# Forming the low halves of the first 80 expert-weight tiles with an accumulating DMA in place of a VectorE subtraction

## The chip, the cores and the metric

The kernel runs on one core of one Trainium2 chip. The metric is the device time of one execution in microseconds (us); lower is better. The engines are TensorE (PE; its weight loads PEld), VectorE (DVE), ScalarE (ACT), GpSimd (POOL) and SyncE (SP), with 16 DMA engines beside them. ACT, POOL and SP also issue DMAs, each on a queue of its own.

## The reference, cut to what matters

The whole program is one block with an SSM branch, an attention branch and a PEER layer, followed by two further blocks, on 512 tokens of width 1024. The change lies in the PEER layer: every token picks 128 of 16384 experts, and each expert is a row of `u_tab` and a row of `v_tab`.

```python
def one_block(args):
    h_blk, i_blk, g_blk = args
    u_sel = u_tab[i_blk]
    act = jax.nn.gelu(jnp.einsum('td,thkd->thk', h_blk, u_sel).astype(jnp.float32))
    w = (g_blk * act).astype(h.dtype)
    return jnp.einsum('thk,thkd->td', w, v_tab[i_blk])
```

## The kernel before, in words

Matrix products are done in fp32r, a rounded fp32, and made exact enough by splitting each operand into a high part (rounded) and a low part (what the rounding lost). `mm3` (L327 to L330) adds three products: high by high (L328), high by low and low by high (L329, L330).

All weights come through one `Stream`. `_load` (L64 to L68) has SP issue the load of a 128x1024 f32 tile `wraw` (512 KB). `_split` (L70 to L77) makes `whi` on ACT (L75, a copy that rounds) and `wlo` on DVE (L76, `wraw - whi`). The tags `wraw`, `whi` and `wlo` have three buffers each. `get` (L79) splits up to two tiles ahead of the one asked for and loads ahead of that. So the split of tile i+2 waits until PE has finished with tile i-1, and the load of tile i+3 waits until tile i is split.

The PEER layer (`peer`, from L915) treats 384 of the tokens densely: for each of 128 tiles of 128 experts it computes the products of all tokens with all rows of U, and weights them with a gate matrix that is zero where an expert was not picked. The other 128 tokens are treated by gathering their rows with indirect DMAs (`gathered`, L965 to L996, an indirect DMA on POOL at L975 and a dot product on DVE at L984).

- The U stage: after the 16 query tiles, `spill(e)` (L1131) runs for e = 0 to 71: one U tile, 24 matmuls (`u_pass`, L960), a Gelu on ACT (L1137) and, every fourth tile, a store of the results to memory (`at`, L1139). Behind each, `tick(0, ...)` (L1144) takes two steps of the gate work, and `tick(1, ...)` a quarter of a step of the gathered lane.
- The gate work: `prep(t)` (L1022) sorts and decodes the picks of 128 tokens, almost all of it on DVE. `build(t)` (L1091) then has 32 steps per block: two comparisons on DVE (L1099, L1100, tiles `o1` and `o2`), a product on POOL (L1101, `og`), eight matmul instructions (L1104) and a copy on ACT (L1105); every eight steps a 2 MB store goes out (L1107, `gt`). The lane does prep(0), prep(1), then build(1) beside prep(2), build(2) beside prep(3), and build(3): 96 build steps in all, and what is left over after e = 71 is drained (L1145).
- Eight late U tiles (L1173, e = 72 to 79) follow, and then the V stage: 128 tiles of V and the 48 remaining tiles of U.

Instructions are placed on each engine's queue in the order of a scheduler's estimate when the program is built, and each engine then works its queue in order. `self.last` (L76) keeps the last low-part subtraction: `tick` ties the DVE instructions of the gathered lane behind it (L1126).

Of the kernel before, what the change touches and what calls it, by code (L numbers as in the profile page):

```python
# [13 lines left out]
AF = mybir.ActivationFunctionType  # L14
ALU = mybir.AluOpType
# [15 lines left out]
N_SPILL = 80  # L31
# [23 lines left out]
class Stream:  # L55
# [14 lines left out]
    def _split(self, i):  # L70
        r = self.raw.pop(i)
        hi = self.pool.tile([P, 1024], F32R, tag="whi", bufs=3, name=f"whi{i}")
        lo = self.pool.tile([P, 1024], F32R, tag="wlo", bufs=3, name=f"wlo{i}")
        w = self.specs[i][3] if len(self.specs[i]) > 3 else 1024
        self.nc.scalar.copy(hi[:, :w], r[:, :w])  # L75
        self.last = self.nc.vector.tensor_sub(lo[:, :w], r[:, :w], hi[:, :w])  # L76
        self.parts[i] = (hi, lo)  # L77

    def get(self, key, ahead=None):  # L79
# [1934 lines left out]
```

## Time and profile before

| | |
|---|---|
| median of 3 runs | 3367.07 us (3360.56 to 3369.22) |
| the profiled execution | 3364.15 us |
| its span, first to last instruction | 3362.4 us |
| granted TensorE clock, mean over the span | 0.977 |
| first U matmul | 584.2 us |
| first and last gate matmul | 730.0 and 1029.0 us |
| first V matmul | 1061.2 us |

Times inside the profile count from the first instruction. The views group instructions by line, engine and shape, with the busy time, the mean of one, and the idle time before it together with what ended it; or they give the busy time of each engine in a stretch. A granted clock of 1.00 is 2.4 GHz, of 0.5 is 1.2 GHz.

### The profile page before, as it was taken

How to read it: one execution, taken by the hardware profiler on the slowest of the kernel's cores; microseconds unless marked ns; L12 is line 12 of the kernel's file. 1: busy time of each engine (PE TensorE's matmuls, PEld its weight loads, DVE VectorE, ACT ScalarE, POOL GpSimd, SP SyncE). 2: the span in 40 equal slices, each digit the busy share in tenths (PEclk: the TensorE clock that was granted, in tenths of full speed). 3: DMA queues.
4: the chain of work that ended last, by engine and by line, in shares of the span. 5: the costliest groups of instructions: out<-in, count | busy, mean ns of one | idle time of the engine just before them, and what ended most of it. 6: DMA issues, size and time to landing. Idle time of an engine off the chain costs nothing.

```text
span 3362.4 us, 46297 instructions
## 1 busy us (share of the span) xinstructions
PE 3174.1 (94%) x17267; PEld 2756.3 (82%) x17267; DVE 2277.1 (68%) x4416; ACT 1344.6 (40%) x2494; POOL 833.3 (25%) x911
## 2 busy tenths in 40 slices
PE   7989999988988999999999996999999999999999
PEld 6988878988987777799998985878888986778887
DVE  6886359999995777788888688743324387753322
ACT  4445233433433333333334454632222377742222
POOL 1451000024554655566664110000000110000000
PEclk9999999999999999999999997999999998999999
DMA  4223332455657999999998221022223210122232
GB/s 139 78 77 112 100 114 85 154 189 200 236 216 277 344 324 332 327 338 335 340 335 295 81 73 42 31 85 97 95 94 130 78 51 1 57 63 95 99 94 82
DMA packets 226417, 529.25 MB, mean 157 GB/s; under 512 B 19080, under 2 KB 113160, under 8 KB 224272
## 3 DMA queue, kind: packets, MB, share of 16 engines
q1 hardware_dynamic: 186448, 376.32, 33.1%
q0 software_dynamic: 36864, 134.23, 11.0%
q10 hardware_dynamic: 2880, 15.73, 1.2%
q8 instruction: 136, 2.23, 0.3%
q14 instruction: 89, 0.73, 0.1%
HBM read 474.17 MB, written 51.40 MB: 156 GB/s over the span
## 4 chain that ended last, share of the span: by engine, by line
PE 56%; DVE 5%; DMA 3%; ACT 2%; issue 1%; POOL 1%; SPq 0%; ACTq 0%; DVEq 0%; POOLq 0%
PE mm L329 15%; PE mm L330 15%; PE mm L328 15%; PE ax L328 2%; PE ax L329 2%; PE ax L330 2%; DMA wraw<-in_peer_v_dram 2%; DVE wlo L76 1%; DMA rw<-in_peer_v_dram,idx 1%; PE tx L1279 1%; PE tx L1839 1%; ACT whi L75 1%; DVE tl L272 1%; PE sx L1819 0%; PE po L1849 0%
## 5 line engine op out<-in xcount | busy, mean ns | idle before, releaser
L76 DVE TENSOR_TENSOR wlo<-wraw,whi 128x1024 fp32r<-128x1024 f32 x525 | 682.6, 1300 | 557.4 <-ACT whi L75 550.7
L75 ACT CAST whi<-wraw 128x1024 fp32r<-128x1024 f32 x525 | 549.6, 1049 | 1056.4 <-PE mm L329 427.6
L330 PE MATMUL mm<-hhi,wlo 128*128 128x512 f32 (+2 forms) x1608 | 597.3, 372 | 6.9 <-DVE wlo L76 6.8
L328 PE MATMUL mm<-hhi,whi 128*128 128x512 f32 (+2 forms) x1608 | 597.5, 373 | 0.1
L329 PE MATMUL mm<-hlo,whi 128*128 128x512 f32 (+2 forms) x1608 | 597.0, 371 | 0.0
L328 PE MATMUL mm<-whi,hhi 128*128 128x256 f32 (+1 forms) x1280 | 381.2, 299 | 10.1 <-DVE vl L272 4.6
L330 PE MATMUL mm<-whi,hlo 128*128 128x256 f32 (+1 forms) x1280 | 379.5, 298 | 2.1 <-DVE hlo L272 1.8
L329 PE MATMUL mm<-wlo,hhi 128*128 128x256 f32 (+1 forms) x1280 | 380.9, 298 | 0.0
L330 PEld LDWEIGHTS mm<-hhi,wlo 128*128 128x128 f32 (+1 forms) x1608 | 302.0, 188 | 48.2 <-DVE wlo L76 7.8
L328 PEld LDWEIGHTS mm<-hhi,whi 128*128 128x128 f32 (+1 forms) x1608 | 302.6, 188 | 41.6 <-ACT hhi L271 0.8
L329 PEld LDWEIGHTS mm<-hlo,whi 128*128 128x128 f32 (+1 forms) x1608 | 302.0, 188 | 40.4 <-DVE hlo L272 0.2
L329 PE MATMUL mm<-wlo,wth 128*128 128x512 f32 x768 | 305.4, 398 | 1.3 <-DVE wlo L76 0.8
L330 PE MATMUL mm<-whi,wtl 128*128 128x512 f32 x768 | 304.6, 397 | 0.0
L328 PE MATMUL mm<-whi,wth 128*128 128x512 f32 x768 | 248.5, 399 | 23.4 <-ACT whi L75 23.4
L975 POOL DMA_INDIRECT rw<-in_peer_rows_dram,idx x128 | 170.1, 1329 | 382.7 <-DVE pk L1066 185.6
L328 PEld LDWEIGHTS mm<-whi,hhi 128*128 128x128 f32 x1280 | 247.2, 193 | 18.4 <-DVE vl L272 4.8
L330 PEld LDWEIGHTS mm<-whi,hlo 128*128 128x128 f32 x1280 | 246.0, 193 | 8.9 <-DVE hlo L272 2.1
L329 PEld LDWEIGHTS mm<-wlo,hhi 128*128 128x128 f32 x1280 | 247.5, 193 | 6.2 <-issue 0.2
L975 POOL DMA_INDIRECT rw<-in_peer_v_dram,idx x128 | 179.6, 1403 | 94.5 <-DVE acc L992 75.2
L328 PEld LDWEIGHTS mm<-whi,wth 128*128 128x128 f32 x768 | 144.3, 189 | 59.8 <-ACT whi L75 29.4
L984 DVE CUSTOM_DVE_ANT_0 rw<-rw,hrow 128x1024 f32<-128x1024 f32 x128 | 176.8, 1389 | 11.1 <-DMA rw<-in_peer_rows_dram,idx 11.1
L992 DVE SCALAR_TENSOR_TENSOR acc<-rw,act,acc 128x1024 f32<-128x1024 f32 x127 | 176.7, 1391 | 11.1 <-DMA rw<-in_peer_v_dram,idx 10.5
(559 smaller groups left out, 5952.8 us busy)
## 6 DMA issues: line engine op xcount, KB each, us to landing
wraw<-in_peer_u_dram SPq DMA_DIRECT2D x128, 512.0 KB, 4.4
wraw<-in_peer_v_dram SPq DMA_DIRECT2D x128, 512.0 KB, 7.0
gt<-gst SPq DMA_DIRECT2D x12, 2048.0 KB, 8.9
g<-gt SPq DMA_DIRECT2D x32, 768.0 KB, 9.3
wraw<-in_w_gate_dram SPq DMA_DIRECT2D x44, 512.0 KB, 3.4
wraw<-in_w_up_dram SPq DMA_DIRECT2D x44, 512.0 KB, 3.4
wraw<-in_w_down_dram SPq DMA_DIRECT2D x44, 512.0 KB, 3.7
at<-as ACTq DMA_DIRECT2D x20, 768.0 KB, 6.5
```

Of the source, the lines that this page charges most:

```text
L75: self.nc.scalar.copy(hi[:, :w], r[:, :w])
L76: self.last = self.nc.vector.tensor_sub(lo[:, :w], r[:, :w], hi[:, :w])
L272: V.tensor_sub(lo, ps, hi)
L328: PE.matmul(ps, ah, bh, start=start, stop=False)
L329: PE.matmul(ps, ah, bl, start=False, stop=False)
L330: PE.matmul(ps, al, bh, start=False, stop=stop)
L975: G.indirect_dma_start(out=rw, out_offset=None, in_=A[("peer_rows", "peer_v")[m]], in_offset=bass.IndirectOffsetOnAxis(ap=idx[:, k:k + 1], ...
L984: V.tensor_tensor_reduce(rw, rw, hrow, 1.0, 0.0, op0=ALU.mult, op1=ALU.add, accum_out=act[:, k:k + 1])
L992: V.scalar_tensor_tensor(acc0, rw, act[:, k:k + 1], acc0, op0=ALU.mult, op1=ALU.add)
L1279: K["nc"].tensor.transpose(ps[:, t * P:(t + 1) * P], src(t), K["ident"])
L1839: PE.transpose(ps[:, (r - j) * P:(r - j + 1) * P], Ps[r][:, j * P:(j + 1) * P], ident)
```

## The change

The low part of U tiles 0 to 79 is formed in two steps. ACT writes the negated weight into `wlo`, which rounds it as it is written, so that `wlo` holds the negated high part. A DMA issued by POOL, from `wraw` to `wlo`, both in on-chip memory, then adds the weight to it. All other tiles keep the subtraction.

```diff
         self.nc.scalar.copy(hi[:, :w], r[:, :w])
-        self.last = self.nc.vector.tensor_sub(lo[:, :w], r[:, :w], hi[:, :w])
+        key = self.specs[i][0]
+        if key[0] == "peer_u" and key[1] < N_SPILL:
+
+            self.nc.scalar.activation(lo[:, :w], r[:, :w], AF.Copy, scale=-1.0)
+            self.nc.gpsimd.dma_start(lo[:, :w], r[:, :w], accum_op=ALU.add)
+        else:
+            self.last = self.nc.vector.tensor_sub(lo[:, :w], r[:, :w], hi[:, :w])
         self.parts[i] = (hi, lo)
```

## Rows read from the trace of the kernel before

**Rows 1.** The page: span, busy engines, and the DVE and DMA slices.

```profile
span 3362.4 us, 46297 instructions
PE 3174.1 (94%) x17267; PEld 2756.3 (82%) x17267; DVE 2277.1 (68%) x4416; ACT 1344.6 (40%) x2494; POOL 833.3 (25%) x911
...
DVE  6886359999995777788888688743324387753322
...
DMA  4223332455657999999998221022223210122232
```

**Rows 2.** PE in order of time: the first matmul of U tile 0.

```profile
584.22 0.33 PE L328 MATMUL mm<-hhi,whi 128*128 128x384 f32 x1
```

**Rows 3.** Busy time by stretch, U stage.

```profile
core 0: us, PE busy (x) PEld busy (x) DVE busy (x) ACT busy (x) POOL busy (x), PEclk, DMA share, GB/s
...
640.00:650.00 10.00, 10.00 (x60) 10.00 (x59) 10.00 (x36) 6.95 (x9) 0.00 (x0) 1.00 0.45 148
...
780.00:790.00 10.00, 8.63 (x57) 8.14 (x55) 10.00 (x15) 4.28 (x7) 3.79 (x4) 1.00 0.47 154
...
980.00:990.00 10.00, 5.80 (x42) 5.24 (x42) 10.00 (x11) 3.67 (x6) 6.92 (x6) 0.94 1.00 402
990.00:1000.00 10.00, 8.02 (x44) 7.43 (x45) 10.00 (x11) 2.93 (x5) 5.69 (x5) 0.72 0.23 96
...
1010.00:1020.00 10.00, 6.78 (x39) 6.06 (x40) 10.00 (x11) 2.34 (x4) 6.65 (x5) 0.80 0.50 211
```

**Rows 4.** Waits by total, 590 to 1030 us (total, times, longest).

```profile
POOL rw L975 <- DVE act L984: 48.8, 8, 15.6
...
PE ax L1104 <- DVE o L1100: 24.4, 33, 1.5
PEld ax L1104 <- POOL og L1101: 21.0, 17, 1.8
```

**Rows 5.** The chain that ended last: the last gate step on PE.

```profile
1028.19 1.14 PE ax L1104 x8
```

**Rows 6.** DMA queues and issues, 560 to 1030 us (KB each, us to landing).

```profile
q1 hardware_dynamic: 12672, 63.44, 37.9%
q10 hardware_dynamic: 2592, 14.16, 7.9%
q0 software_dynamic: 2736, 9.96, 6.3%
...
wraw<-in_peer_u_dram SPq DMA_DIRECT2D x77, 512.0 KB, 3.8
gt<-gst SPq DMA_DIRECT2D x12, 2048.0 KB, 8.9
```

**Rows 7.** Groups by line, 560 to 1030 us.

```profile
L1101 POOL TENSOR_TENSOR og<-o,sl 128x512 f32<-128x512 f32 x96 | 148.6, 1561 | 129.1 <-PE ax L1104 74.9 <-DVE o L1099 38.7 <-ACT as L1137 11.1
...
L76 DVE TENSOR_TENSOR wlo<-wraw,whi 128x1024 fp32r<-128x1024 f32 x77 | 100.6, 1307 | 7.2 <-ACT whi L75 7.2
...
L975 POOL DMA_INDIRECT rw<-in_peer_rows_dram,idx x19 | 25.5, 1340 | 241.3 <-DVE pk L1066 185.6 <-DVE act L984 48.8 <-DVE bp L1050 2.7
```

**Rows 8.** ACT in order of time: two successive U tiles without gate work.

```profile
707.08 1.05 ACT L75 CAST whi<-wraw 128x1024 fp32r<-128x1024 f32 x1 [2.72 <-PE mm L329]
...
711.24 1.05 ACT L75 CAST whi<-wraw 128x1024 fp32r<-128x1024 f32 x1 [2.72 <-PE mm L329]
```

**Rows 9.** Groups by line, 590 to 728 us (before the gate matmuls).

```profile
L76 DVE TENSOR_TENSOR wlo<-wraw,whi 128x1024 fp32r<-128x1024 f32 x29 | 35.5, 1223 | 0.0
L75 ACT CAST whi<-wraw 128x1024 fp32r<-128x1024 f32 x31 | 32.6, 1052 | 78.6 <-PE mm L329 66.4 <-DVE pk L1066 7.5 <-DMA wraw<-in_peer_u_dram 3.2
```

**Rows 10.** The gathered row tile, 560 to 1030 us.

```profile
DMA to landing us min/median/max: 4.9/7.9/11.7
```

**Rows 11.** The loads of U, 560 to 1030 us (ns min/median/max).

```profile
L67 SPq DMA_DIRECT2D wraw<-in_peer_u_dram x77: 327/328/328, 561.1 to 986.5; - x77
```

**Rows 12.** The gate matmuls, first and last start (us).

```profile
L1104 PE MATMUL ax<-og,o x768: 271/275/553, 730.0 to 1029.0; 128*128 128x128 f32 x192
```

**Rows 13.** DMA issues, 1060 to 1700 us (the V stage).

```profile
wraw<-in_peer_u_dram SPq DMA_DIRECT2D x36, 512.0 KB, 6.5
```

## The prediction

> **What bounds the kernel now.** I read the page first, then the stage of the change by stretches, then groups, DMA and waits. On the page PE is busy 94% of the span, so over the whole kernel PE looks like the bound; but six of DVE's slices in a row show nines, 504 to 1009 us, and the tiles in question are worked from 584 us on [rows 1, 2]. The stretches settle it. At 640 us PE and DVE are both full; at 780 DVE is full and PE is at 8.63 of 10; from 980 to 1030 DVE is full and PE at 5.8 to 8.0, with a granted clock of 0.72 to 0.94 (a mix of 2.4 and 1.2 GHz, after PE had begun to idle) [rows 3]. In that last stretch the U tiles are done and PE only runs gate matmuls as DVE delivers their comparisons: PE waited 24.4 us for L1100 and its weight loads 21.0 us for the product on POOL that is made from it [rows 4]. So DVE sets the end of the U stage (first U matmul at 584.2 us [rows 2], last gate matmul ending at 1029.3 [rows 5]), and the late tiles and the V stage stand behind it. DMA is not the bound in the U stage: its three large queues are busy 37.9 + 7.9 + 6.3 = 52% [rows 6].
>
> **The change, part by part.**
>
> *DVE loses the subtractions.* There are 77 of them in the stage, 1.307 us each, 100.6 us in all [rows 7]. DVE, now full for most of 445 us (1029.3 - 584.2), would need some 345. What is late next is PE: 72 tiles at 4.16 us (the distance of two successive tiles, 711.24 - 707.08 [rows 8]) make 300 us, 96 gate steps at 1.14 us [rows 5] make 109, two batches of query scores 2 and small transposes 1 more; together 412. So no more than 445 - 412 = **33 us** can be won, whatever DVE saves.
>
> *ACT gains 80 passes.* The nearest row is the rounding copy of the same shape, 1.05 us [rows 9]: 84 us. ACT is busy 3 to 7 us of 10 [rows 3], so they find room; but each now stands in the path of its tile, which the ring below counts. Without that cover they would be 84 us.
>
> *POOL gains 80 DMA issues.* The nearest row: an indirect DMA holds POOL 1.34 us [rows 7]; 107 us in all. POOL is at most 7 us busy in 10 while the gates are built [rows 3], so this too fits, with some 1.6 us to spare in a tile of 6.43 us that has two products of 1.56 us [rows 7] (3.1 + 1.3 + 0.3 for a quarter of a gather). Behind the waiting issue stand the products, which PE's gate matmuls need, and the gathers; ahead of it may stand a gather that itself waits for a dot product on DVE (48.8 us in 8 waits, the longest 15.6 [rows 4]). DVE will be less late, so I price that at nothing and keep up to 30 us (two long waits) for the range. The dot products lose their tie to the subtractions of these tiles: zero for the same reason. SP issues as many loads as before, but each now waits for a landing in place of a subtraction.
>
> *The accumulating DMA itself.* The trace has none. From below: the plain load of 512 KB lands in 3.8 us [rows 6]. From above: two gathers one after the other, 2 x 7.9 = 15.8 us [rows 10]. It is nearest to a gather (same issuer, same size), but must read 512 KB from each of two places, so I take a gather plus one more 512 KB of engine time: a gather's is 6.3% of 470 us over 19 = 1.56 us [rows 6], and 7.9 + 1.5 = **9.4 us** from issue to landing.
>
> The Trainium skill, page "DMA: Bandwidth & Descriptors", section "Anatomy of one DMA", puts a DMA issued by GpSimd at 2.0 us plus its bytes at 436 GB/s, by which I estimate 3.2 us for 512 KB; with it the sum would be the full gain. The gathers here took 4.9 to 11.7 us [rows 10], so the trace doesn't bear that out for this stage. The same page, "Rules for kernel authors", says that an accumulating DMA reads its destination and writes it later; no run here shows it.
>
> *The ring.* With three buffers a tile must be split, released and reloaded within three tiles of PE time: copy 1.05, negation 1.05, DMA 9.4, the load's issue 0.33 [rows 11] and its landing 3.8 = 15.6 us for three tiles, so one every **5.2 us**. Counted through `wlo` it is the same: 4.16 for the tile, some 2.4 for two passes, 9.4: 16 us. Where a tile carries two gate steps PE needs 4.16 + 2.28 = 6.43 us and the ring is hidden; where it carries none, PE waits 1.04 us per tile. Tiles without gates come at two places.
> - Early: until the first gate matmul. That was at 730 us [rows 12], 146 us after the first U matmul, of which subtractions took 35.5 in the part from 590 on [rows 9] and some 2 before; 108 us remain, in which PE idles 1.04/5.2, a fifth: **+21 us**.
> - Late: the lane takes two steps per tile and some 133 steps (37 of prep, 96 of build), so it is done near tile 66; with the eight late tiles 14 are without gates: 14 x 1.04 = **+15 us**.
>
> *DMA engines in the gate phase* (some 48 tiles). A tile brings a load, 1.5 us of all engines (37.9% of 470 us for 63.44 MB is 356 GB/s [rows 6]), 0.5 for `at` (7.9% of 470 over 72), 1.3 for `gt` (25 MB at the 402 GB/s of [rows 3] over 48) and 0.5 for gathers: 3.8. An accumulation that reads and writes in step costs 1.56 us like a gather, then 5.4 of 6.43 is used and nothing is lost; one that reads 1 MB at 402 GB/s costs 2.6, which makes 6.4, a full engine. Then landings lengthen as in the V stage, where the same load takes 6.5 us in place of 3.8 [rows 6, 13]; with 2.7 us more on load and DMA the ring needs (15.6 + 5.4)/3 = 7.0 us per tile, 0.57 over PE, 27 us in 48 tiles. I take the middle of none and 27: **+14 us**.
>
> **Sum.** -33 + 21 + 15 + 14 = +17 us on the profiled execution: 3364.2 + 17 = 3381. That execution lies 2.9 us under the median of the three runs, so I give **3384 us**. About 0.3% (10 us) is what a measurement of this kernel can tell from no change.
>
> **The rivals.**
> - *The landing is short (faster).* The same ring hides the DMA entirely if it lands in 12.5 - 6.2 = 6.3 us or less. For: the quickest gather took 4.9 us [rows 10], and this one needn't read from off-chip memory. Against: 7.9 is the median. Then PE is the bound and the 33 us are won: 3367 - 33 = 3334 us; a landing of 7.5 gives (6.2 + 7.5)/3 = 4.6 us, losses of 10 and 6, 3350. The fixed-cost rule of the Trainium skill above would give this. Chance 0.34. Its bound is a landing of 8.3 us: there a tile takes 4.85 us, and losses of 15 and 10 leave 8 us.
> - *They cancel (no change).* Landing 8.3 to 10 us and no queue in the gate phase: at 9.1 us a tile takes 5.1 us, and 20 + 13 us are lost of 33. 3357 to 3377. Chance 0.16.
> - *The two reads follow each other (much slower).* Landing 15.8 us: the ring takes (6.2 + 15.8)/3 = 7.3 us for every tile, gates or not; 80 tiles make 587 us where they now take about 479 (445 for 72, eight more at 4.16): 108 us more, 3475. With loads at 6.5 us it is 8.2 us a tile and 3547. For: the DMA engines also carry the loads and the 2 MB stores (landing 8.9 us [rows 6]); against: no 512 KB gather took more than 11.7. It decides from a landing of 13 us on, where the ring exceeds the 6.43 us of a tile with gates. Chance 0.14.
> - That the change doesn't do what it says is no case of its own: the subtraction is gone for these 80 tiles whatever the DMA takes. If DVE's comparisons (1.56 us beside them on POOL) slowed by what they gain, the second case would come out, and is counted there.
>
> **How the numbers follow.** My forecast, slower by the ring's wait at the places without gates, has chance 0.36 and a range of its own of 3377 to 3430 (landing 9 to 12 us, with and without the queue). The range 3334 to 3480 reaches from the full gain to the doubled landing and leaves out the V entry coming still earlier below, and a saturated DMA above. Faster by over 0.3%: 0.34; within 0.3%: 0.16; slower: 0.36 + 0.14 = 0.50.
>
> **What would show it.** Right: DVE below 8 of 10 in the U stage; ACT's copies waiting for the load of `wraw`, and PE for the DMA into `wlo`, in the first 100 us after 584 and around the end of the stage; tiles 5 to 6 us apart there; the accumulations landing in 9 to 10 us; the stretch of gates without U tiles at 980 to 1030 gone. Wrong: accumulations landing within 6 us and tiles 4.2 us apart (first rival); tiles over 6.5 us apart also while gates are built, with the DMA share near 1 (third rival); or PE waiting for products on POOL that stand behind a DMA issue, which I priced at nothing.

## The result, and the profile after

The changed kernel took **3406.31 us** (median of 4 runs, 3403.49 to 3410.91), against 3364.28 us for the kernel before on the same chip. The ratio is 1.0123 [1.0111, 1.0136]: slower by 42 us, where 17 were forecast. The direction held, the size did not. (Below, the bracket behind a ratio is its 95% interval. Ratios are turned into microseconds by 3366 us; the intervals then reach some 4 to 8 us to either side.) In the lines of after, everything behind the split stands 6 lines lower: L1110 is the gate matmul that was L1104, L1107 the product `og`, L981 the gather, L990 its dot product. L79 and L80 are the new negation and the new DMA.

The page of the changed kernel, its span, engines and two of its slices (85 us each; the U stage is the 7th to the 13th digit):

```profile
span 3401.6 us, 46430 instructions
PE 3189.1 (94%) x17267; PEld 2772.9 (82%) x17267; DVE 2168.3 (64%) x4336; ACT 1415.9 (42%) x2574; POOL 894.5 (26%) x991
DVE  6886359897560777888888788743323377753323
DMA  4223233998999989999999321123224210113232
```

The row of nines that DVE had in the U stage [rows 1] now breaks off after three digits (9 8 9 7 5 6 0), and the nines stand with the DMA engines instead, which points to them and to what waits on them. The stretches of the same kernel say where (length, then busy time and instructions of PE, PEld, DVE, ACT and POOL, then the granted clock, DMA share and GB/s):

```profile
584.00:655.00 71.00, 64.83 (x351) 63.67 (x350) 64.65 (x367) 44.82 (x54) 11.67 (x14) 0.93 0.90 221
655.00:740.00 85.00, 60.37 (x302) 56.36 (x301) 72.19 (x164) 30.39 (x39) 42.08 (x37) 0.88 0.96 281
740.00:810.00 70.00, 60.30 (x387) 56.15 (x386) 69.97 (x87) 34.20 (x50) 40.86 (x31) 1.00 0.82 232
810.00:1025.00 215.00, 205.99 (x1357) 204.72 (x1356) 127.52 (x138) 111.81 (x167) 127.23 (x102) 0.98 0.95 277
```

The same stretches of the kernel before:

```profile
584.00:655.00 71.00, 71.00 (x416) 70.96 (x415) 70.79 (x369) 35.73 (x46) 0.00 (x0) 1.00 0.44 149
655.00:740.00 85.00, 75.29 (x426) 73.81 (x426) 79.07 (x128) 25.63 (x36) 18.66 (x13) 0.96 0.59 200
740.00:810.00 70.00, 61.99 (x384) 58.29 (x383) 70.00 (x120) 26.56 (x40) 30.91 (x19) 1.00 0.52 180
810.00:1025.00 215.00, 197.86 (x1286) 191.99 (x1284) 207.69 (x219) 84.63 (x133) 122.03 (x84) 0.96 0.57 213
```

PE was full in the first 71 us and now idles 6 of them; in the next 85 it idles 24.6 where it idled 9.7, and the granted clock is 0.88 (a mix of the two levels, 2.4 and 1.2 GHz) where it was 0.96. From 740 to 810 us little changes. In the long stretch PE is busier than before (206.0 of 215 us, before 197.9) and DVE no longer full (127.5, before 207.7), with the DMA engines at 0.95. So PE lost its time early in the stage, and again on the late tiles (below). The transfers from 560 to 1070 us of the changed kernel (queues: packets, MB, share of the engines; issues: count, KB each, median us to landing), and the landing of the new DMA by itself, 560 to 1090 us:

```profile
q0 software_dynamic: 13680, 49.81, 47.3%
q1 hardware_dynamic: 13831, 65.61, 35.4%
wraw<-in_peer_u_dram SPq DMA_DIRECT2D x76, 512.0 KB, 4.9
wlo<-wraw POOLq DMA_DIRECT2D x76, 512.0 KB, 7.3
gt<-gst SPq DMA_DIRECT2D x12, 2048.0 KB, 11.9
...
L80 POOL DMA_DIRECT2D wlo<-wraw x78: 835/872/1311, 574.3 to 1088.2; - x78
DMA to landing us min/median/max: 4.5/7.3/13.5
```

Queue q0, which had 6.3% [rows 6], holds 47.3% of the engines' time: 241 us of 510. Less 19 gathers of 1.56 us (the prediction's figure), 212 us are left for 76 accumulations, **2.8 us each**. The 2 MB gate stores land after 11.9 us instead of 8.9, the loads after 4.9 instead of 3.8 [rows 6].

The waits of the changed kernel, 590 to 1030 us (total, times, longest):

```profile
ACT whi L75 <- DMA wraw<-in_peer_u_dram: 98.9, 25, 9.4
POOL og L1107 <- PE ax L1110: 81.7, 44, 4.7
POOL wlo L80 <- ACT wlo L79: 79.6, 21, 9.2
DVE o L1106 <- PE ax L1110: 73.9, 59, 5.9
...
PEld mm L336 <- DMA wlo<-wraw: 28.5, 14, 5.0
PE mm L336 <- DMA wlo<-wraw: 24.7, 13, 4.7
```

Now DVE waits for PE, not PE for DVE as before [rows 4]. ACT's rounding waits for late loads, 25 times and up to 9.4 us, and PE for the new DMA. The end of the stage, in the changed kernel and then in the one before (ns min/median/max, first and last start; the low-by-high product of the first 72 U tiles, then the V stage):

```profile
L335 PE MATMUL mm<-hlo,whi x607: 331/334/525, 560.6 to 1053.9; 128*128 128x384 f32 x144, 128*128 128x512 f32 x8
L1110 PE MATMUL ax<-og,o x768: 271/275/582, 720.7 to 1031.0; 128*128 128x128 f32 x192
L334 PE MATMUL mm<-whi,wth x768: 388/393/793, 1110.1 to 1873.0; 128*128 128x512 f32 x192
```

```profile
L329 PE MATMUL mm<-hlo,whi x589: 331/334/522, 574.7 to 981.0; 128*128 128x384 f32 x192, 128*128 128x512 f32 x5
L328 PE MATMUL mm<-whi,wth x768: 387/393/797, 1061.2 to 1834.2; 128*128 128x512 f32 x192
```

The gates end where they did (1031.0, before 1029.0 [rows 12]), but the U tiles, which were through at 981.0 and left the gates alone behind them, now end at 1053.9. The 72 tiles and all 96 gate steps together thus take 25 us longer than before, and the eight late tiles with the entry to the V stage (1053.9 to 1110.1, before 1029.0 to 1061.2) another 24. The V stage starts 49 us later and ends 39 us later; the V stage itself is 10 us shorter.

Two places show what came to stand in the way. First POOL's queue, together with ACT and DVE, 674 to 694 us (start, us, line, and in brackets the idle time before and what ended it):

```profile
681.68 1.45 POOL L981 DMA_INDIRECT rw<-in_peer_rows_dram,idx  x1 [4.10 <-DVE act L990]
683.84 1.06 ACT L79 ACTIVATE wlo<-wraw 128x1024 fp32r<-128x1024 f32 x1
685.80 1.44 POOL L981 DMA_INDIRECT rw<-in_peer_rows_dram,idx  x1 [2.67 <-DVE act L990]
686.21 1.05 ACT L79 ACTIVATE wlo<-wraw 128x1024 fp32r<-128x1024 f32 x1
689.91 0.94 POOL L981 DMA_INDIRECT rw<-in_peer_rows_dram,idx  x1 [2.66 <-DVE act L990]
690.85 1.92 POOL L80 DMA_DIRECT2D wlo<-wraw  x2
```

Two tiles were negated by 684.9 and 687.3, and both accumulations were issued at 690.85: ahead of them on POOL stood gathers that each waited for a dot product on DVE to give back a row buffer. Second, the chain that ended last around two gate stores (start, us, what), which SP issued at 903.1 and 929.4:

```profile
900.37 5.08 DMA wlo<-wraw
905.46 16.20 DMA wraw<-in_peer_u_dram
...
928.01 5.57 DMA wlo<-wraw
933.59 13.96 DMA wraw<-in_peer_u_dram
```

At these two of the twelve stores, the load that had to wait for an accumulation ran beside the 2 MB store and landed after 14 to 16 us. ACT's rounding then waits 9 us for it, and two successive tiles stand 12.6 us apart:

```profile
935.03 1.05 ACT L75 CAST whi<-wraw 128x1024 fp32r<-128x1024 f32 x1 [2.21 <-DMA wraw<-in_peer_u_dram]
947.63 1.04 ACT L75 CAST whi<-wraw 128x1024 fp32r<-128x1024 f32 x1 [9.25 <-DMA wraw<-in_peer_u_dram]
```

### The profile page after: what moved, and what is told of

It reads as the page before. It is cut to its first block, busy times and chain, and to the rows that moved or that the text cites. A ratio compares the mean times of both kernels' runs of the same rounds, so it can differ in the third digit from the quotient of the medians.

```text
span 3401.6 us, 46430 instructions
## 1 busy us (share of the span) xinstructions
PE 3189.1 (94%) x17267; PEld 2772.9 (82%) x17267; DVE 2168.3 (64%) x4336; ACT 1415.9 (42%) x2574; POOL 894.5 (26%) x991
## 4 chain that ended last, share of the span: by engine, by line
PE 68%; DVE 12%; DMA 9%; issue 5%; ACT 3%; POOL 3%; SPq 0%; POOLq 0%; DVEq 0%; ACTq 0%
PE mm L335 18%; PE mm L336 18%; PE mm L334 18%; DMA wraw<-in_peer_v_dram 2%; DMA wlo<-wraw 2%; DMA wraw<-in_peer_u_dram 2%; PE ax L334 2%; PE ax L336 2%; PE ax L335 2%; DVE wlo L82 2%; POOL og L1107 2%; DMA rw<-in_peer_rows_dram,idx 1%; PE tx L1285 1%; ACT whi L75 1%; DVE ei L1073 1%
## 5 line engine op out<-in xcount | busy, mean ns | idle before, releaser
L82 DVE TENSOR_TENSOR wlo<-wraw,whi 128x1024 fp32r<-128x1024 f32 x445 | 570.0, 1281 | 548.2 <-ACT whi L75 541.6
L336 PE MATMUL mm<-hhi,wlo 128*128 128x512 f32 (+2 forms) x1608 | 604.5, 377 | 25.9 <-DMA wlo<-wraw 25.7
L334 PE MATMUL mm<-hhi,whi 128*128 128x512 f32 (+2 forms) x1608 | 606.3, 378 | 3.8 <-ACT whi L75 3.6
L981 POOL DMA_INDIRECT rw<-in_peer_rows_dram,idx x128 | 168.1, 1313 | 169.0 <-DVE act L990 152.2
L981 POOL DMA_INDIRECT rw<-in_peer_v_dram,idx x128 | 184.6, 1442 | 101.0 <-DVE acc L998 77.5
L1171 ACT CAST wth<-w 128x384 fp32r<-128x384 f32 x128 | 65.7, 514 | 290.7 <-PE mm L335 177.9
L990 DVE CUSTOM_DVE_ANT_0 rw<-rw,hrow 128x1024 f32<-128x1024 f32 x128 | 173.7, 1365 | 18.8 <-DMA rw<-in_peer_rows_dram,idx 18.8
## 6 DMA issues: line engine op xcount, KB each, us to landing
gt<-gst SPq DMA_DIRECT2D x12, 2048.0 KB, 11.9
```

The source lines that it names most:

```text
L334: PE.matmul(ps, ah, bh, start=start, stop=False)
L336: PE.matmul(ps, al, bh, start=False, stop=stop)
L981: G.indirect_dma_start(out=rw, out_offset=None, in_=A[("peer_rows", "peer_v")[m]], in_offset=bass.IndirectOffsetOnAxis(ap=idx[:, k:k + 1], ...
L990: V.tensor_tensor_reduce(rw, rw, hrow, 1.0, 0.0, op0=ALU.mult, op1=ALU.add, accum_out=act[:, k:k + 1])
L1171: S.copy(wh, w)
```

## The experiments

All diffs are against the changed kernel.

### What the DMA costs, in three steps

**Without it.**

```diff
-            self.nc.gpsimd.dma_start(lo[:, :w], r[:, :w], accum_op=ALU.add)
```

> The changed kernel without the accumulating DMA: the low part of the 80 tiles is left as the negated high part. It leaves out the addition. It prices what DVE's freed time is worth with the transfer at nothing. By the prediction's first term (PE needs 412 us of the 445) it should take 3364 - 33 = 3331 us, with U tiles 4.2 us apart until the gates begin. If another thing than the transfer held the changed kernel up (the second pass on ACT, the order of the dot products), it would stay above 3355.

Measured: 3322.47 us, 0.9865 [0.9849, 0.9882], 9 us under the forecast of this run. Everything else of the change is still there (the subtraction gone, ACT's 80 passes), so it is worth 45 us, and what ACT's passes may cost is contained in that. Its stretches:

```profile
655.00:740.00 85.00, 73.62 (x434) 71.60 (x432) 82.17 (x178) 43.44 (x57) 32.19 (x27) 0.94 0.72 263
810.00:1025.00 215.00, 209.04 (x1387) 208.72 (x1386) 125.94 (x130) 123.46 (x176) 96.85 (x67) 0.99 0.64 236
```

PE is the bound again (209 of 215 us). The V stage starts at 1024.6, 37 us earlier than before; the forecast bound of 33 us was sound as far as that point, and some 8 us more come behind it.

**A plain copy in its place.**

```diff
-            self.nc.gpsimd.dma_start(lo[:, :w], r[:, :w], accum_op=ALU.add)
+            self.nc.gpsimd.dma_start(lo[:, :w], r[:, :w])
```

> The same DMA without the addition: it copies the weight over the negated value (the low part is then wrong). Same issuer, queue, waits and bytes written, but one place read in place of two. If the engine time of the accumulation (about 2.8 us of all 16 engines for 512 KB in the changed kernel) is what counts, the copy holds them about 1.5 us, the U stage is no longer short of DMA, and the time falls to 3335 to 3355. If it is the chain of issue and landing through three buffers whatever the transfer does, landings stay near 7 us and the time stays above 3385.

Measured: 3371.78 us, 1.0015 [1.0004, 1.0027], between the two expectations: engine time counts, but not alone. The transfers, 560 to 1070 us:

```profile
q0 software_dynamic: 14112, 51.39, 28.5%
...
wlo<-wraw POOLq DMA_DIRECT2D x80, 512.0 KB, 5.6
```

The queue takes 145 us of 510; less 19 gathers, 116 us for 80 copies, 1.45 us each. The same bytes written with an addition take the engines 2.8 us, 1.9 times as long, and land 1.7 us later (7.3).

**An eighth of it.**

```diff
-            self.nc.gpsimd.dma_start(lo[:, :w], r[:, :w], accum_op=ALU.add)
+            self.nc.gpsimd.dma_start(lo[:, :w // 8], r[:, :w // 8], accum_op=ALU.add)
```

> The change with the DMA cut to the first 128 of 1024 columns; the other columns of the low part stay the negated high part. Every issue, wait and place on POOL's queue stays, the engine time shrinks to about an eighth (0.35 us). If engine time is what cost, the time comes to within 12 us of the run without the DMA: 3322 to 3335. If DMA issues standing behind gathers on POOL's queue cost as well (in the changed kernel two were issued at 690.9 us whose inputs were ready at 684.9 and 687.3), they go on costing: 3340 to 3365.

Measured: 3344.74 us, 0.9942 [0.9919, 0.9965], the second expectation. Its second stretch, and the landing of its 64 KB:

```profile
655.00:740.00 85.00, 69.02 (x393) 66.86 (x393) 84.80 (x180) 39.01 (x52) 50.70 (x42) 0.94 0.78 264
DMA to landing us min/median/max: 2.3/3.2/8.7
```

Where its first loss comes from can be read directly, 645 to 664 us (in order of time):

```profile
646.16 1.05 ACT L79 ACTIVATE wlo<-wraw 128x1024 fp32r<-128x1024 f32 x1
649.76 1.56 POOL L981 DMA_INDIRECT rw<-in_peer_rows_dram,idx  x1 [5.56 <-DVE idx L1077]
655.55 1.01 POOL L80 DMA_DIRECT2D wlo<-wraw  x1
662.30 0.69 PE L336 MATMUL mm<-hhi,wlo 128*128 128x384 f32 x1 [7.40 <-DMA wlo<-wraw]
```

A tile was negated at 647.2, but its small DMA was issued 8.3 us later: POOL stood waiting with the first gather for its indices from DVE, and issued four gathers first. PE then idled 7.4 us for it. This is POOL's queue with little else: the transfer takes 0.5 us of the engines' time.

The four kernels make a ladder of the DMA's whole cost of 87 us (42 + 45): that 80 small ones are there at all, in the path of each tile and behind the gathers on POOL, 26 us (0.9942 - 0.9865); that they carry 512 KB, 25 us more (1.0015 - 0.9942); that they add, 36 us more (1.0123 - 1.0015). The steps are not quite clean: a copy also holds POOL for less time than a DMA that adds (0.57 us in place of 0.87).

### Where the cost falls

**Only from tile 20 on, and only below tile 72.** The rest goes by subtraction.

```diff
-        if key[0] == "peer_u" and key[1] < N_SPILL:
+        if key[0] == "peer_u" and 20 <= key[1] < N_SPILL:
```

> Three buffers, DMA only for tiles 20 to 79: it prices the early places. The prediction gave them 21 us. If the early tiles' waits are a loss: 3380 to 3395. If not, because DVE's decoding of picks then comes later by the subtractions it takes back (20 x 1.22 = 24 us): 3400 to 3412.

```diff
-        if key[0] == "peer_u" and key[1] < N_SPILL:
+        if key[0] == "peer_u" and key[1] < N_SPILL - N_LATE:
```

> Three buffers, as changed, but the eight late tiles keep the subtraction: it prices the late places by themselves. The prediction gave the late tiles 15 us (14 tiles x 1.04). In the changed kernel the last gate matmul was at 1031 and the first V matmul at 1110, against 1029 and 1061 before. If that stretch is lost to the late tiles' DMAs: 3370 to 3385. If it is lost because the U tiles before it are late: 3393 to 3406.

Measured: 3383.5 us, 1.0040 [1.0024, 1.0056], and 3393.64 us, 1.0074 [1.0053, 1.0095]. Leaving out the first 20 tiles thus gives back 28 us (1.0123 - 1.0040, the first expectation), leaving out the last eight 16 (1.0123 - 1.0074, at the edge of the second expectation). By difference 43 of the 87 us are left for the tiles between. But that is no price of the work beside the gates, as the traces show when the tiles are counted in them (start of the first matmul, us, U tiles numbered from 0; in brackets the gate steps done by then):

| | U tile 20 | U tile 30 | U tile 72 | V stage |
|---|---|---|---|---|
| before | 669.2 | 720.9 (0) | 1030.0 | 1061.2 |
| without the DMA | 669.0 | 729.6 (6) | 993.5 | 1024.6 |
| an eighth of it | 679.7 | 743.4 (10) | 1001.6 | 1043.1 |
| the changed kernel | 701.5 | 780.9 (17) | 1053.7 | 1110.1 |
| DMA only from tile 20 on | 670.5 | 758.8 (8) | 1038.6 | 1093.4 |
| no gathers (next run) | 690.3 | 753.1 (16) | 1013.1 | 1071.5 |
| four sets (below) | 681.5 | 753.3 (14) | 1008.8 | 1049.2 |

Against the kernel without the DMA the changed one is 32 us late at tile 20. At tile 30 it is 39 us late (51.3, less 11 gate steps more of 1.14 us), at tile 72, with all gates done, 60, and at the V stage 85. So **39 of the 85 us fall before tile 30**, 21 on tiles 30 to 71, beside the gates, and 25 on the late tiles and the entry to the V stage. In the run from tile 20 on, the loss of the early places did not go away; much of it moved. Its 19 gathers go out from 669.9 to 726.5 us, beside the first tiles with a DMA, and it loses 25 us between tile 20 and tile 30, where the changed kernel loses 6.

**No gathers during the U stage** but for the four that fill the row buffers (one run); the others move to the V stage.

```diff
-DOTS_C = 20
+DOTS_C = 0
```

> The change with the 20 early steps of the gathered lane moved behind the U stage, so that no gather stands on POOL's queue between the DMA issues of the U stage. The V stage becomes longer for it (20 more gathers), so the U stage alone is read, up to the first V matmul (1110 us in the changed kernel, 1061 before). If DMA issues behind gathers cost the stretch 655 to 740 (60 of 85 us busy on PE): first V matmul at 1070 to 1090, and PE over 70 of 85. If it is the engines' time alone, the 19 gathers' 30 us are saved on them and no more: 1085 to 1105.

```profile
655.00:740.00 85.00, 76.16 (x436) 73.44 (x437) 80.07 (x167) 43.53 (x58) 33.60 (x30) 0.94 0.94 257
```

Measured: 3390.18 us, without an interval. PE is busy 76.2 of these 85 us again (60.4 with the gathers, 75.3 before), though the DMA engines are as full (0.94); the V stage starts at 1071.5 instead of 1110.1. So most of what was lost in this stretch was lost to the gathers: by the table 11 of the 32 us until tile 20, 27 of the 39 until tile 30 (one gate step counted), and 39 at the V stage. Not all of it need be POOL's queue. The transfers of 15 gathers went too, 15 x 1.56 = 23 us of engine time, and with them 15 dot products of 1.2 us on DVE, which the sorting for the gates had to make room for in that stretch.

**The tie of the dot products kept,** by a one-column copy on DVE per tile.

```diff
             self.nc.gpsimd.dma_start(lo[:, :w], r[:, :w], accum_op=ALU.add)
+            mk = self.pool.tile([P, 1], F32, tag="mk", bufs=3, name=f"mk{i}")
+            self.last = self.nc.vector.tensor_copy(mk, hi[:, :1])
```

> The change as it is, with one small DVE copy per tile (128x1) to which the dot products of the gathered lane are tied as they were to the subtraction. In the changed kernel the first 19 gathers went out between 655 and 725 us, before 9 by 738. If that bunching (10 x 1.56 us of engine time and waits on POOL) costs the stretch 655 to 740 its 9 lost tiles, the time falls by 15 to 30 us, to 3376 to 3390; if not it stays within 8 us of 3406.

Measured: 3417.43 us, 1.0142 [1.0124, 1.016], 11 us above the changed kernel (6 by the ratios), which is neither expectation. In the stretch named PE does get 11 us back (busy 71.8 of 85; seven gathers go out there and not 19), but from 810 to 1025 us, where the gathers now stand, it is busy 196.0 of 215 where it was 206.0. The time lost behind the gathers moves with them; the lost tie does not explain it.

### Buffers

**A fourth set** of `wraw`, `whi` and `wlo` needs memory, which a third gate buffer gives up. So there is a control with that alone.

```diff
-                    st = tp.tile([P, NE, 32], F32, tag="gst", bufs=3, name=nm("gst"))
+                    st = tp.tile([P, NE, 32], F32, tag="gst", bufs=2, name=nm("gst"))
```

> Control for the next run: the change with two buffers in place of three for the gate tile that is stored to memory, which makes room on chip. Both theories: within 10 us of the change, 3400 to 3420.

```diff
+    def _tile(self, i, dt, tag):
+        key = self.specs[i][0]
+        if key[0] == "peer_u" and key[1] < N_SPILL and key[1] % 4 == 3:
+            return self.pool2.tile([P, 1024], dt, tag=tag + "4", bufs=1, name=f"{tag}{i}")
+        return self.pool.tile([P, 1024], dt, tag=tag, bufs=3, name=f"{tag}{i}")
...
-        r = self.pool.tile([P, 1024], F32, tag="wraw", bufs=3, name=f"wraw{i}")
+        r = self._tile(i, F32, "wraw")
...
-        hi = self.pool.tile([P, 1024], F32R, tag="whi", bufs=3, name=f"whi{i}")
-        lo = self.pool.tile([P, 1024], F32R, tag="wlo", bufs=3, name=f"wlo{i}")
+        hi = self._tile(i, F32R, "whi")
+        lo = self._tile(i, F32R, "wlo")
```

> The change with four sets of wraw, whi and wlo for the 80 tiles in place of three (every fourth tile has a set of its own), and two gate tiles as in the control. If the ring of three buffers is what waits, a tile gets 4.2 us more for the same chain: at a landing of 7.3 and a load of 4.9 us the ring is (2.1 + 7.3 + 0.3 + 4.9)/4 = 3.7 us a tile, under PE's 4.2, and the time falls to 3365 or below. If the 16 DMA engines are short of time (they were 0.90 to 1.02 busy from 584 us to 1100), more tiles in flight only queue: within 12 us of the control.

Measured: the control 3402.15 us, 1.0099 [1.008, 1.0118]; four sets 3363.55 us, 0.9986 [0.9975, 0.9996]. The long stretch, first of the control, then of four sets:

```profile
810.00:1025.00 215.00, 203.86 (x1341) 202.27 (x1340) 127.13 (x138) 111.86 (x167) 127.80 (x102) 0.98 0.93 275
```

```profile
810.00:1025.00 215.00, 212.71 (x1410) 212.15 (x1409) 128.50 (x129) 124.77 (x175) 115.86 (x102) 1.00 1.00 295
```

The fourth set takes 39 us back while the engines are fuller still (1.00) and the accumulations land later (8.2 us in the median, up to 15.3). So full DMA engines were not the whole of the limit; a ring of three was too short to ride out what came late. These two rows show only 9 of the 39 us. By the table above four sets are 20 us ahead of the changed kernel at tile 20 already, and 45 at tile 72. With the last eight tiles by subtraction as well:

> Four sets of buffers, the DMA for all of the first 72 tiles and the subtraction for the eight late ones. If the late tiles' DMAs cost near the entry to the V stage (the engines were 1.06 busy there): 10 to 20 us under the four-set run of 3364. If the late tiles are hidden with four sets: 3358 to 3368.

Measured: 3340.99 us, 0.9925 [0.991, 0.994], below both expectations, 50 us better than the same choice of tiles with three sets (1.0074) and 25 better than the kernel before.

### Both routes side by side

**Every second tile,** of all 80 and of the first 72; then two of three.

```diff
-        if key[0] == "peer_u" and key[1] < N_SPILL:
+        if key[0] == "peer_u" and key[1] < N_SPILL and key[1] % 2:
```

> Only every second of the 80 tiles takes the DMA, the others the subtraction on DVE. If DMA engine time is the bound, 40 x 2.8 = 112 us are saved on the engines and the stage is bound by PE again, with DVE at some 375 of 412 us: 3335 to 3360, perhaps below the kernel before. If each DMA tile costs a wait of its own whatever the others do, half of the 42 us remain: about 3385.

```diff
-        if key[0] == "peer_u" and key[1] < N_SPILL:
+        if key[0] == "peer_u" and key[1] < N_SPILL - N_LATE and key[1] % 2:
```

> Every second of the first 72 tiles takes the DMA; the eight late tiles, which have no gate work on DVE beside them, keep the subtraction. If the engine time near the entry of the V stage counts (the engines were 1.04 busy there with every second tile), it beats the every-second run of 3343 us by 3 to 8: 3335 to 3340. If not, 3340 to 3348.

> Two of three of the first 72 tiles take the DMA, three buffers. Against every second tile (3339 us) it frees 12 more subtractions (15 us of DVE) and adds 12 x 2.8 = 34 us of engine time. If the ring of three with long landings is the limit, two DMA tiles in a row wait again: 3345 to 3365. If DVE still bound the gate phase with every second tile: below 3335.

Measured: 3343.2 us, 0.9923 [0.9906, 0.994]; **3339.14 us, 0.9919 [0.9905, 0.9934]**; and for two of three (`key[1] % 3` in the last diff) 3351.05 us, 0.9949 [0.9934, 0.9964]. The first two cannot be told apart; two of three is some 10 us slower. The second of them, in the stretches where the changed kernel lost:

```profile
655.00:740.00 85.00, 78.61 (x462) 76.77 (x461) 83.85 (x178) 37.94 (x52) 34.85 (x27) 0.98 0.85 255
...
810.00:1025.00 215.00, 209.26 (x1377) 207.78 (x1376) 176.97 (x173) 104.40 (x155) 110.70 (x93) 0.98 0.83 271
DMA to landing us min/median/max: 4.5/6.0/9.4
```

Half of the subtractions gone is enough to take DVE off the bound in the long stretch (177 of 215 us busy), the DMA engines keep a sixth free there, and no landing is over 9.4 us. The subtractions that stay also keep the gathers tied: nine go out between 655 and 740 us, as before, and not 19. By the ratios this kernel is 27 us (0.8%) faster than the one before and 69 faster than the changed one, and level with four sets for the first 72 tiles.

**What could add to that.** Four sets and every second tile, and every second tile without gathers in the U stage (the diffs are those above put together):

> Four sets of buffers and the DMA for every second of the first 72 tiles. If the ring no longer waits with every second tile (landing 6.0 us), the fourth set adds nothing: 3333 to 3345. If it still does: 3320 to 3333.

> Every second of the first 72 tiles by DMA, and no gathers in the U stage. If the V stage's DMA-bound pace makes up for 20 more gathers no better than before, it costs 20 x 1.56 = 31 us there and gains at most 20 in the U stage: 3340 to 3355. If the V stage hides them: 3325 to 3337.

Measured: 3340.07 us, 0.9928 [0.9914, 0.9942], no further gain, as expected where the ring no longer waits; and 3369.39 us, 1.0003 [0.9991, 1.0015], 28 us worse and above both expectations. There the V stage starts at 1039.5 (1035.3 with the gathers), but the last of its gathered rows is added at 1839.1 us and not at 1796.4: for the gathers, which got in front of the weights in the U stage, the V stage was no better place.

## Why the prediction was right or wrong

- **The bound before** was read rightly: with the subtraction gone and nothing in its place, PE fills the stage (209 of 215 us) and DVE waits for PE. (The waits of 24.4 and 21.0 us that it puts into the last stretch are those of 590 to 1030 us; from 980 on they are 14.7 and 14.3.)
- **The gain, forecast at most -33,** was -45: -37 at the start of the V stage, the rest behind it, where no term looked.
- **ACT's 80 passes at nothing:** held, in the kernel without the DMA. **The tie of the dot products at nothing:** putting it back won nothing in the whole time, though without it the gathers bunched (19 between 655 and 740 us, before nine).
- **The early places, +21:** the ring did what was forecast, and without gathers the tiles are 21 us late at tile 20 (690.3 against 669.0). That the size agrees is partly luck: the landing was shorter than forecast (7.3 for 9.4 us) and the load's longer (4.9 for 3.8). With both the prediction's ring takes 4.9 us a tile and not 5.2, and in the changed kernel the tiles came 4.8 us apart until 647 us (11 of them in 53.1 us).
- **POOL's queue at nothing is the step that failed.** The issues hold POOL 0.87 us each, not 1.34. But "ahead of it may stand a gather that itself waits for a dot product on DVE" was priced at nothing, because DVE would be less late. It came about all the same: the issues at 690.85 stood 4 to 6 us behind their input, DVE was still busy 72 of the 85 us from 655 to 740, and with a transfer of 0.5 us of engine time the queue still made PE idle 7.4 us (an eighth of the DMA). Before tile 30 the changed kernel lost 39 us and not 21, and 27 of them came back without the gathers (more than the 18 missing, for the kernel without the DMA, which has its gathers, is held up there too: PE waits 9.7 us for DVE). How much of this is POOL's queue alone stays open. The 30 us kept for the range would have been the better choice.
- **A lower clock** is part of these 39 us: up to 740 us PE idled 31 us, without the DMA 11, but it also had a granted clock of 0.93 and 0.88, without the DMA 1.00 and 0.94. My estimate from these figures is 10 us (0.07 of 71 and 0.06 of 85). The prediction had no term for it.
- **The gate phase, +14,** came to 21 us (tiles 30 to 71), inside the prediction's own "none and 27". The engine time of an accumulation, 1.56 to 2.6 us there, was 2.8, above both ends. By the prediction's list 3.8 + 2.8 = 6.6 us of transfers stand against 6.43 of PE, so the upper end was the likelier. **The late places, +15,** were 16 by the time of the run without them, 25 by the traces.
- **The landing, 9.4 us,** was 7.3 in the median. By the prediction's own first rival a landing of 7.5 us makes the kernel 17 us faster; it came out 42 us slower. The median did not describe this ring of three: landings went from 4.5 to 13.5 us, and the loads of two chains took 14 to 16. ACT waited 98.9 us for loads, PE 24.7 for accumulations. Four sets, which give a late transfer more time and take no load off the engines, took 39 us back.
- **The signs named** came in part: ACT's copies wait for `wraw` and PE for `wlo`, and no gates stand alone behind the U tiles any more; but DVE is under 8 of 10 only from 810 us on and still full from 740 to 810 (70 of 70), where PE idles 9.7 us.
- **The Trainium skill's** estimate of 3.2 us (page "DMA: Bandwidth & Descriptors", section "Anatomy of one DMA") is met by no accumulation of 512 KB here (4.5 to 13.5 us); a plain copy came as low as 2.9, with a median of 5.6. The remark of its section "Rules for kernel authors" that an accumulating DMA also reads its destination agrees with the 1.9-fold engine time.
- **The sum by the traces:** -37 + 39 + 21 + 25 = 48 us at the start of the V stage (49 measured), where -33 + 21 + 14 + 15 = 17 were forecast. Of the miss, 18 us lie before tile 30, 10 on the late tiles and 7 beside the gates, less 4 by the greater gain. The V stage then gave 10 us back. Of the rivals, the third (the two reads follow each other) had the DMA share near 1 right (0.95), but not the doubled landing; and the tiles beside the gates, 6.5 us apart, stand 6.3 apart without the DMA as well.

Left open: how the gathers' cost divides between POOL's queue, their transfers and their dot products on DVE; and why the V stage itself is 10 us shorter in the changed kernel, for which no run was made.

## What to carry to other kernels

The DMA that took over an engine's pass here was paid three times: in the DMA engines' time (for one that adds, about twice that of a copy), in a landing that joins the path of its tile, and in the queue of the engine that issues it, behind whatever waits there. So look at what stands in that queue before pricing it at nothing. Price the ring by the longest landings beside the largest transfer, not by the median, and see whether one more buffer rides them out. If an engine is only somewhat too full, try relief on every second tile: here half of the change was worth 27 us and the whole of it cost 42, while a fourth set of buffers made all of the first 72 tiles worth 25. And when an experiment leaves tiles out, count in the trace whether the loss went away or moved to another place.

## What the runs showed of the hardware that was not expected

- 512 KB within on-chip memory: 2.8 us of the 16 engines' time when adding, 1.45 us when copying, both worked out from the queue's share; without the gathers the same sum for adding gives 2.7 (43.9% of 510 us, less four gathers, over 80). An eighth of it, adding, takes 0.5 us (16.2% of 510 us, less 27 gathers, over 80), more than an eighth of 2.8.
- Landings in median, least and most: adding 512 KB 7.3 (4.5 to 13.5), copying it 5.6 (2.9 to 12.1), adding 64 KB 3.2 (2.3 to 8.7).
- The issue holds POOL 0.87 us for one that adds and 0.57 us for a copy (medians), and it waits its turn: 8.3 us behind four gathers in the run with an eighth of the DMA.
